# A hybrid decoder layer: recurrence rows moved by DMA, token sums asked for earlier, gate sigmoids kept apart from the decays' exponentials

## The chip, the cores and the metric

The kernel runs on one core of a Trainium2 chip. The core has five engines that run side by side, each with its own queue in a fixed order: TensorE (PE in the profile; it multiplies matrices into banks of PSUM), VectorE (DVE), ScalarE (ACT; it applies functions from tables that it loads), GpSimd (POOL) and SyncE (SP, which here only issues DMAs). They meet at semaphores. The metric is the device time of one execution in microseconds (us); the numbers given are the median of several runs.

## The reference, cut to what matters

One decoder layer on 512 tokens of width 1024, all in float32. A normalised input is projected once into everything that three token mixers and their gates need; the mixers are a gated recurrence with a short convolution (branch 0), chunked gated linear attention (branch 1) and cross-attention to a memory (branch 2). Each mixer's output is projected to the model width, multiplied by a sigmoid gate of its own, and the three are added.

```python
z = rms_norm(x, norm_mix) @ w_in
z_rnn, z_q, z_k, z_v, z_g, z_dec, z_mq, z_gate = split(z)
out_a = rg_lru(causal_dwconv(z_rnn), ...)            # a, u per channel; h_t = a_t h_(t-1) + u_t
log_alpha = log_sigmoid(z_dec @ w_decay + b_decay) / 16
o_gla = chunked_gla(z_q, z_k, z_v, log_alpha)        # cumulated decays, exponentials of them
out_b = rms_norm(o_gla) * silu(z_g)
out_c = softmax(q_mem k_mem / sqrt(d)) v_mem
merged = sum_n sigmoid(z_gate[n]) * (out_n @ w_branch[n])
x = x + merged @ w_out                               # then a gated MLP, and a final norm
```

## The kernel before, in words

**Three matmuls for one.** Every large product is made in a short float format: an operand is split into a high part (a ScalarE copy, L96) and a low part (a VectorE subtraction, L97), and `mm3` (L99) adds hi x hi, hi x lo and lo x hi into one PSUM bank. So each weight block costs a DMA, a ScalarE and a VectorE operation before TensorE can use it. Its high and low parts live in three buffers each (`whi`, `wlo`, NWB = 3), the raw block in four.

**Units and steps.** The program is written down as a list (`prog`) of *units*, weight blocks with their matmuls, and *steps*, other work. `emit` (L182) goes through the list. A unit can ask for functions to be called some units earlier: its load and split two units before (AHEAD = 2), others by the numbers in `pre`. `weave` (L150) spreads steps evenly over units, `blend` (L343) lays the units of a fast product between others. A planner then orders each engine's queue: by the order of the program, but an operation that is ready by the planner's own costs may go ahead of one that isn't. Activations live in 53 slots of 2 KB per partition (`fslot`, `rslot`), and a bank of five in PSUM (`bank`) holds a product until it is read.

**The stage of the change.** Branch 2's units come first, with the recurrence in the steps between: `lru_decay`, `lru_root` and, per block of 96 channels, `lru_scan` (L700), a scan along the tokens on VectorE. Blocks 4 to 7 do not fit the 128-row layout of the projection, so each is cut into three pieces of 32 rows, which ScalarE copies to other partitions (L716, twelve in all). When one of the six tiles is full it is split for TensorE (`oa`).

Then `v_fast` and `g_fast` make the values and the gate of branch 1 by a scheme with seven half-size products in place of eight (`seven`, L284; a1, a2, c1, c2, b1, b2, b3, each of two units). Weights are summed by accumulating DMAs on GpSimd's queue (L298). Sums of token halves are made on VectorE from the normalised input: `h_quarter` (L757) puts a quarter together, `h_sum1` and `h_sum4` (L767, L772) subtract and add them, and `h_ready` splits the result in the same call. `h_sum1` is asked for four units before c1, `h_sum4` five before c2, `h_sum23` four before b1. `v_read` (L794) and `g_read` (L825) empty the banks after each product: L801 and L804 on ScalarE, L805, L809 and the rest on VectorE. `g_read` also calls `silu` (L819), a sigmoid and a product. Seven units of branch 0, gate units (24 matmuls and a sigmoid, L619) and product units (18 matmuls and two VectorE operations, L627 and L628), lie among them: gate 0, gate 1, product 0, product 1, gate 2, product 2, gate 3.

The rest of branch 0 and two held gates of branch 1 (`hold`, L997; sigmoid at L1000) are woven with the decays: `decay_in`, `qk_back` (eight loads of queries and keys by GpSimd), `decay_logit`, `decay_log` (exponentials L883, logarithms L886) and `decay_apply` (L890), which sums the decays along the tokens (L897 to L900) and takes four exponentials per head (L904 to L907) to scale queries and keys (L908 to L913). Six more held gates carry the chunked attention: `k_end` (transposes, L920), `intra`, `state`, `gla_out`, `gla_norm`, `gla_flip`. At the end come the eight products of branch 1.

Of the kernel before, what the change touches and what calls it, by code (L numbers as in the profile page):

```python
# [13 lines left out]
AF = mybir.ActivationFunctionType  # L14
# [4 lines left out]
P = 128  # L19
D = 1024  # L20
KD = D // P
S = 512
NT = S // P
MEM = 256
NMT = MEM // P
MIX = 768
NM = MIX // P
H = 4
DK = 96
# [27 lines left out]
def trunk(ctx: ExitStack, tc: tile.TileContext, x, xT, mem, memT, par, wdecay, wch, wv, wg, wmk,  # L57
# [17 lines left out]
    def fslot(shape=(P, S)):  # L75
        return apool.tile(list(shape), F32, tag="s", name=nm("f"))

    def rslot(shape=(P, S)):
        return apool.tile(list(shape), F32R, tag="s", name=nm("r"))
# [14 lines left out]
    def split(hi, lo, src, eng=None):  # L94

        nc.scalar.activation(hi, src, AF.Copy)  # L96
        (eng or nc.vector).tensor_tensor(out=lo, in0=src, in1=hi.bitcast(F32), op=ALU.subtract)  # L97
# [423 lines left out]
    def proj_in(i, evac):  # L521
        return wch[i], D, lambda w: evac(channel_major(w, KD, lambda k: (hh[:, k, :], hl[:, k, :])))
# [90 lines left out]
    def branch(n, acts, d, gt=None):  # L613

        g = [gt]

        def gate(ps):
            g[0] = fslot()
            nc.scalar.activation(g[0], ps, AF.Sigmoid)  # L619

        def proj(w):
            pp = channel_major(w, NM, lambda k: acts[k])
            if n == BRANCHES[0]:
                merged.append(mslot())
                nc.vector.tensor_tensor(out=merged[d], in0=pp, in1=g[0], op=ALU.mult)
                return
            nc.vector.tensor_tensor(out=g[0], in0=pp, in1=g[0], op=ALU.mult)  # L627
            nc.vector.tensor_tensor(out=merged[d], in0=merged[d], in1=g[0], op=ALU.add)  # L628
            if n == BRANCHES[2]:
                r = (rslot(), rslot())  # L630
                split(*r, merged[d])
                mr.append(r)
        return [proj_in(18 + 8 * n + d, gate), (wbr[n, d], MIX, proj)]
# [66 lines left out]
    def lru_scan(b):  # L700
        a, w = lru.pop(("aw", b))
        gi = lru.pop((1, b))
        nc.vector.tensor_tensor(out=gi, in0=gi, in1=xr[b], op=ALU.mult)
        nc.vector.tensor_tensor(out=w, in0=w, in1=gi, op=ALU.mult)
        if b < 4:
            of.append(fslot())
            gi = of[b][:DK]
        nc.vector.tensor_tensor_scan(out=gi, data0=a, data1=w, initial=0.0, op0=ALU.mult, op1=ALU.add)
        if b < 4:
            return  # L710
        for r in range(3):
            i = 3 * (b - 4) + r
            t, o = (i, DK) if i < 4 else (i // 4 + 3, 32 * (i % 4))
            if t >= 4 and o == 0:
                of.append(fslot())
            nc.scalar.activation(of[t][o:o + 32, :], gi[32 * r:32 * r + 32, :], AF.Copy)  # L716
            if o == DK:
                rr = (rslot(), rslot())
                split(*rr, of[t])
                oa.append(rr)  # L720

    each = lambda fn, bs: [lambda b=b: fn(b) for b in bs]
    lo, hi = range(4), range(4, 8)
# [33 lines left out]
    def h_quarter(r, c, p):  # L757
        f = hsum["f", r, c, p] = fslot((P, 2, HT))
        a, b = (v[:, 4 * c - 4 + 2 * p:4 * c - 2 + 2 * p, (r - 1) * HT:r * HT].bitcast(F32) for v in (hh, hl))
        nc.vector.tensor_tensor(out=f, in0=a, in1=b, op=ALU.add)  # L760
        return f

    def h_ready(key, p, a):
        hsum[key, p] = rslot((P, 2, HT)), rslot((P, 2, HT))
        split(*hsum[key, p], a)

    def h_sum1(p):  # L767
        a, b = h_quarter(2, 1, p), h_quarter(2, 2, p)
        nc.vector.tensor_tensor(out=b, in0=a, in1=b, op=ALU.subtract)
        h_ready("c1", p, b)  # L770

    def h_sum4(p):  # L772
        tt = nc.vector.tensor_tensor
        a, b, s3, s1 = h_quarter(1, 1, p), h_quarter(1, 2, p), hsum["f", 2, 1, p], hsum["f", 2, 2, p]
        tt(out=s3, in0=a, in1=s3, op=ALU.subtract)
        tt(out=a, in0=s1, in1=a, op=ALU.subtract)
        tt(out=b, in0=b, in1=a, op=ALU.add)
        h_ready("c2", p, b)

    def h_sum23(p):  # L780
        h_ready("b1", p, hsum["f", 1, 1, p])
        h_ready("b2", p, hsum["f", 2, 1, p])

    def h_lhs(key, p, j, i):
        tk = slice(i * P, (i + 1) * P)
# [30 lines left out]
            tt(out=flat2(vt[2 + i][0]), in0=k[:, :HP], in1=z, op=ALU.add)  # L816
            tt(out=gla["zd"][:, 2 + i, :], in0=k[:, HP:], in1=ps[:, HP:], op=ALU.add)

    def silu(t, hp, z):  # L819
        s = fslot((P, 2, DV))  # L820
        nc.scalar.activation(flat2(s), z, AF.Sigmoid)
        nc.vector.tensor_tensor(out=flat2(s), in0=flat2(s), in1=z, op=ALU.mult)
        sg[t][hp] = s

    def g_read(key, i, z):  # L825
        tt = nc.vector.tensor_tensor
        if key == "a1":
            gla["g", i] = fslot((P, HP))
            nc.scalar.activation(gla["g", i], z, AF.Copy)
        elif key == "a2":  # L830
            silu(i, 0, z)
        elif key in ("c1", "c2"):
            d = gla["g", key, i] = fslot((P, HP))
            tt(out=d, in0=z, in1=gla["g", i], op=ALU.subtract)
        elif key in ("b1", "b2"):
            d = gla.pop(("g", "c2" if key == "b1" else "c1", i))
            tt(out=d, in0=d, in1=z, op=ALU.subtract)
            silu(i if key == "b1" else i + 2, 1, d)
        else:
            d = gla.pop(("g", i))  # L840
            tt(out=d, in0=d, in1=z, op=ALU.add)
            silu(i + 2, 0, d)

    def v_fast():
        return seven(lambda q, p: wv[p, int(q[1]) - 1, int(q[2]) - 1], HP + LOW, 2, h_lhs,
                     {"c1": [(4, h_sum1)], "c2": [(5, h_sum4)], "b1": [(4, h_sum23)]}, v_read, 4)

    def g_fast():
        return seven(lambda q, p: wg[p, int(q[1]) - 1, int(q[2]) - 1], HP, 2, h_lhs, {}, g_read, 4)
# [39 lines left out]
    dec = const.tile([DK, H, NT], F32, name="dec")  # L889
    qi = []  # L890

    def decay_apply(h):


        by_chunk = lambda a: a.rearrange("p (n c) -> p n c", c=P)
        at = lambda a, i: by_chunk(a)[:, :, i:i + 1].broadcast_to([DK, NT, P])
        nc.vector.tensor_tensor(out=gc[h], in0=gc[h], in1=ea[h], op=ALU.subtract)  # L897
        g = ea[h]
        nc.vector.tensor_tensor_scan(out=g, data0=chm, data1=gc[h], initial=0.0, op0=ALU.mult, op1=ALU.add)
        nc.vector.tensor_tensor(out=by_chunk(gc[h]), in0=at(g, P - 1), in1=by_chunk(g), op=ALU.subtract)  # L900
        m, e, q2 = fslot((DK, S)), fslot((DK, S)), fslot((DK, S))
        nc.vector.tensor_tensor(out=by_chunk(m), in0=by_chunk(g), in1=at(g, CH - 1), op=ALU.subtract)
        with tc.issue_after(gla["last"].ins):
            nc.scalar.activation(gc[h], gc[h], AF.Exp, scale=IG)  # L904
            nc.scalar.activation(q2, g, AF.Exp, scale=IG)
            nc.scalar.activation(e, m, AF.Exp, scale=IG)
            nc.scalar.activation(m, m, AF.Exp, scale=-IG)  # L907
        nc.vector.tensor_tensor(out=gc[h], in0=gc[h], in1=ks[h][:DK], op=ALU.mult)  # L908
        nc.vector.tensor_copy(dec[:, h, :], by_chunk(q2)[:, :, P - 1])
        nc.vector.tensor_tensor(out=q2, in0=q2, in1=qs[h][:DK], op=ALU.mult)  # L910
        qi.append(q2)
        nc.vector.tensor_tensor(out=qs[h][:DK], in0=qs[h][:DK], in1=e, op=ALU.mult)
        nc.vector.tensor_tensor(out=ks[h][:DK], in0=ks[h][:DK], in1=m, op=ALU.mult)  # L913
# [77 lines left out]
        ob.append((hi, lo))  # L991

    step(causal)
    b0 = [u for d in range(KD) for u in branch(0, oa, d)]
    gates = {}

    def hold(d):  # L997
        def evac(ps):
            gates[d] = fslot()
            nc.scalar.activation(gates[d], ps, AF.Sigmoid)  # L1000
        return proj_in(18 + 8 + d, evac)

    held = [hold(d) for d in range(KD)]

    b0 = b0[0:3:2] + [b0[i] for i in range(16) if i not in (0, 2)]
    blend(b0[:7], v_fast() + g_fast())
    weave(b0[7:] + held[:2], [decay_in, qk_back] + [lambda h=h: decay_logit(h) for h in range(H)] + [decay_log] +
          [lambda h=h: decay_apply(h) for h in range(H)])
    tiles = range(NT)
    for u, steps in zip(held[2:], (  # L1010
            each(k_end, tiles) + each(intra, range(H)),
            [lambda n=n, hp=hp: state(n, hp) for n in range(2) for hp in range(2)],
            [lambda hp=hp: state(2, hp) for hp in range(2)] + [lambda t=t: gla_out(t, 0) for t in tiles],
            [lambda: gla_norm(0)] + [lambda t=t: gla_out(t, 1) for t in tiles],
            each(gla_flip, range(3)) + [lambda: gla_norm(1)],
            each(gla_flip, range(3, 6)))):
        weave([u], steps)
    for d in range(KD):
        def late(w, d=d):
            branch(1, ob, d, gates.pop(d))[1][2](w)  # L1020
        weave([(wbr[1, d], MIX, late)], [])


    x2 = [[None, None] for _ in range(NT)]
# [309 lines left out]
```

## Time and profile before

| | us |
|---|---|
| median of 3 runs | 949.54 (948.67 to 950.61) |
| the profiled execution | 949.42 |
| its span, first to last instruction | 947.7 |
| mean granted TensorE clock | 0.993 |
| TensorE busy | 925.9 (98%) |
| VectorE busy | 636.8 (67%) |
| ScalarE busy | 500.4 (53%) |
| GpSimd busy | 83.0 (9%) |

Shares are means over stages with different limits. The rows shown in the prediction have these forms. A *wait* names who waited for whom, then the total, the number of times and the longest. A *group* names line, engine, operation, output<-input, shapes and count, then busy us and mean ns of one, then the engine's idle time before them and what ended it. A *timeline* row gives start, duration and the operation, and in brackets the idle time before it. A row of the *table of stretches* gives the stretch, its length, and busy us (count) of PE, PEld, DVE, ACT and POOL, then granted clock, DMA share and GB/s.

### The profile page before, as it was taken

What the parts mean: (1) busy time and instruction counts of PE and PEld (TensorE: products, weight loads), DVE (VectorE), ACT (ScalarE), POOL (GpSimd) and SP (SyncE); (2) the same over time, 40 slices, a digit from 0 to 9 for tenths busy, and PEclk for the clock granted to TensorE, in tenths of its full rate; (3) what the DMA queues carried; (4) which work ended last, traced back from release to release, by engine and by line L of the source; (5) the groups of instructions that cost most, each with busy time, mean ns of one, the idle gap of its engine ahead of it and who ended that gap; (6) DMA issues with size and microseconds to landing.
All of it is one profiled execution on the core that took longest, in us unless ns stands there. A gap on an engine that the chain in (4) does not pass through costs nothing.

```text
span 947.7 us, 12014 instructions
## 1 busy us (share of the span) xinstructions
PE 925.9 (98%) x4414; PEld 782.4 (83%) x4414; DVE 636.8 (67%) x1111; ACT 500.4 (53%) x806; POOL 83.0 (9%) x115
## 2 busy tenths in 40 slices
PE   8999999999987999999999999999999999999996
PEld 6899888888876998788988898888888888888885
DVE  7897745565777565496767675555585766689765
ACT  7665555584964344696434424433445445445544
POOL 0000000000013151000000000000020221012102
PEclk9999999999998999999999999999999999999999
DMA  7445223223349594322136601323454685357712
GB/s 253 154 124 195 91 77 99 86 72 118 89 99 194 114 217 140 103 71 71 35 117 218 204 17 39 102 90 107 159 104 142 135 222 132 112 114 188 165 45 89
DMA packets 45115, 116.09 MB, mean 122 GB/s; under 512 B 5297, under 2 KB 12609, under 8 KB 45057
## 3 DMA queue, kind: packets, MB, share of 16 engines
q1 hardware_dynamic: 33088, 94.23, 30.5%
q0 software_dynamic: 11392, 20.06, 12.7%
q10 hardware_dynamic: 576, 1.05, 0.3%
q8 instruction: 34, 0.56, 0.2%
q14 instruction: 25, 0.20, 0.1%
HBM read 111.65 MB, written 3.67 MB: 122 GB/s over the span
## 4 chain that ended last, share of the span: by engine, by line
PE 88%; ACT 5%; DVE 5%; issue 1%; DMA 0%; SPq 0%; DVEq 0%; ACTq 0%
PE mm L103 81%; PE sm L103 3%; DVE wlo L97 1%; ACT f L716 1%; PE mm L413 1%; ACT whi L96 1%; DVE r L97 1%; PE sm L957 1%; ACT r L96 0%; DMA m<-in_xT 0%; PE sm L943 0%; PE sm L959 0%; ACT L619 0%; DVE m L381 0%; PE sm L930 0%
## 5 line engine op out<-in xcount | busy, mean ns | idle before, releaser
L97 DVE TENSOR_TENSOR wlo<-raw,whi 128x1024 fp32r<-128x1024 f32 (+2 forms) x155 | 172.0, 1113 | 157.8 <-ACT whi L96 70.1
L96 ACT ACTIVATE whi<-raw 128x1024 fp32r<-128x1024 f32 (+2 forms) x155 | 150.0, 970 | 162.0 <-PE mm L103 148.9
L103 PE MATMUL mm<-whi,r 128*128 128x512 f32 (+2 forms) x568 | 171.9, 373 | 0.0
L103 PE MATMUL mm<-h2l,whi 128*128 128x512 f32 x360 | 140.1, 389 | 0.0
L103 PE MATMUL mm<-h2h,whi 128*128 128x512 f32 x360 | 139.9, 389 | 0.0
L103 PEld LDWEIGHTS mm<-whi,r 128*128 128x128 f32 x568 | 106.4, 189 | 15.4 <-issue 0.3
L103 PE MATMUL mm<-hh,whi 128*128 128x512 f32 x288 | 114.7, 398 | 3.0 <-ACT whi L96 3.0
L103 PE MATMUL mm<-hl,whi 128*128 128x512 f32 x288 | 113.7, 395 | 0.0
L103 PE MATMUL mm<-wlo,r 128*128 128x512 f32 (+2 forms) x284 | 106.3, 374 | 0.2 <-DVE wlo L97 0.2
L103 PE MATMUL mm<-r,whi 128*128 128x512 f32 (+1 forms) x448 | 100.3, 373 | 6.3 <-DVE f L805 6.3
L103 PEld LDWEIGHTS mm<-r,whi 128*128 128x128 f32 x448 | 78.6, 191 | 21.4 <-issue 7.4
L103 PE MATMUL mm<-h2h,wlo 128*128 128x512 f32 x360 | 88.9, 389 | 0.0
L96 ACT ACTIVATE whi<-f 128x512 fp32r<-128x512 f32 (+2 forms) x90 | 48.2, 580 | 74.9 <-PE mm L103 62.9
L97 DVE TENSOR_TENSOR wlo<-f,whi 128x512 fp32r<-128x512 f32 (+2 forms) x90 | 53.9, 632 | 38.4 <-PE mm L103 21.1
L103 PEld LDWEIGHTS mm<-h2h,wlo 128*128 128x128 f32 x360 | 67.6, 188 | 14.0
L103 PEld LDWEIGHTS mm<-h2l,whi 128*128 128x128 f32 x360 | 67.6, 188 | 14.0
L103 PEld LDWEIGHTS mm<-h2h,whi 128*128 128x128 f32 x360 | 67.5, 188 | 13.9
L1098 DVE SCALAR_TENSOR_TENSOR f<-mm,prm,f 128x511 f32<-128x511 f32 x96 | 71.4, 745 | 6.9 <-ACT f L1096 6.1
L298 POOL DMA_DIRECT2D f<-in_wdown x40 | 35.2, 981 | 435.9 <-DMA f<-in_wdown 290.9
L103 PE MATMUL mm<-hh,wlo 128*128 128x512 f32 x288 | 71.9, 390 | 0.0
L103 PEld LDWEIGHTS mm<-hh,whi 128*128 128x128 f32 x288 | 54.7, 190 | 15.2 <-ACT whi L96 3.3
L103 PEld LDWEIGHTS mm<-hl,whi 128*128 128x128 f32 x288 | 54.7, 190 | 11.1
(233 smaller groups left out, 1317.4 us busy)
## 6 DMA issues: line engine op xcount, KB each, us to landing
raw<-in_wup SPq DMA_DIRECT2D x48, 512.0 KB, 3.6
raw<-in_wch SPq DMA_DIRECT2D x40, 512.0 KB, 3.5
f<-in_wdown POOLq DMA_DIRECT2D x40, 256.0 KB, 5.5
raw<-in_wbr SPq DMA_DIRECT2D x24, 384.0 KB, 3.2
raw<-in_wdown SPq DMA_DIRECT2D x14, 512.0 KB, 3.6
f<-in_wdown SPq DMA_DIRECT2D x20, 256.0 KB, 5.0
raw<-in_wout SPq DMA_DIRECT2D x8, 512.0 KB, 3.5
f<-in_wv POOLq DMA_DIRECT2D x16, 200.0 KB, 5.0
```

What stands on the lines that cost most here:

```text
L96: nc.scalar.activation(hi, src, AF.Copy)
L97: (eng or nc.vector).tensor_tensor(out=lo, in0=src, in1=hi.bitcast(F32), op=ALU.subtract)
L103: nc.tensor.matmul(ps, lhsT=l, rhs=r, start=first and i == 0, stop=last and i == len(seq) - 1, skip_group_check=more)
L298: nc.gpsimd.dma_start(raw[to, p][j], src(q, p)[:, j, :], accum_op=ALU.add)
L413: nc.tensor.matmul(ps[u], lhsT=a, rhs=b, start=q == 0 and i in (0, 2), stop=q == KD - 2 and i >= len(seq) - 2)
L716: nc.scalar.activation(of[t][o:o + 32, :], gi[32 * r:32 * r + 32, :], AF.Copy)
L957: nc.tensor.matmul(ps[:, j, :], lhsT=sT[h][:, t, :], rhs=vt[t][hp][:, j, :], start=True, stop=t == 0)
L1098: nc.vector.scalar_tensor_tensor(out=a[:, j:], in0=ps[:, :S - j], scalar=col(C_FCW + 48 * (2 - j) + f), in1=a[:, j:], op0=ALU.mult, op1=AL ...
```

## The change

- `lru_scan` moves its pieces with twelve DMAs on GpSimd's queue in place of ScalarE copies. The splits become steps of their own (`lru_out`), three behind product a2 and three behind product c2 of `v_fast`.
- `h_sum1` and `h_sum4` only make the sums, and are asked for seven units before c1 and c2. `h_ready` is asked for two units before c1, c2, b1 and b2; `h_sum23` is gone.
- `g_read` leaves the gate's input in slots; `silu` is called in the state stage, four times behind `intra` and four times ahead of the last `state`.
- Gate 2 and product 1 change places. Gates 4 to 7 of branch 0 come together, woven with `decay_in`, logits, logarithms and the decays' sums (`decay_sum`, taken out of `decay_apply`); products 3 to 7 follow, woven with `qk_back` and `decay_apply`. All eight held gates of branch 1 carry the chunked attention, whose steps are spread over eight units in place of six.

```diff
-            nc.scalar.activation(of[t][o:o + 32, :], gi[32 * r:32 * r + 32, :], AF.Copy)
-            if o == DK:
-                rr = (rslot(), rslot())
-                split(*rr, of[t])
-                oa.append(rr)
+            nc.gpsimd.dma_start(of[t][o:o + 32, :], gi[32 * r:32 * r + 32, :])
+
+    def lru_out(t):
+        oa.append((rslot(), rslot()))
+        split(*oa[t], of[t])
...
-    def h_ready(key, p, a):
-        hsum[key, p] = rslot((P, 2, HT)), rslot((P, 2, HT))
+    def h_ready(key, p):
+        a, hsum[key, p] = hsum[key, p], (rslot((P, 2, HT)), rslot((P, 2, HT)))
         split(*hsum[key, p], a)
...
         a, b = h_quarter(2, 1, p), h_quarter(2, 2, p)
+        hsum["c1", p] = b
         nc.vector.tensor_tensor(out=b, in0=a, in1=b, op=ALU.subtract)
-        h_ready("c1", p, b)
...
-        h_ready("c2", p, b)
-
-    def h_sum23(p):
-        h_ready("b1", p, hsum["f", 1, 1, p])
-        h_ready("b2", p, hsum["f", 2, 1, p])
+        hsum["c2", p], hsum["b1", p], hsum["b2", p] = b, a, s3
...
-    def silu(t, hp, z):
+    def silu(t, hp):
+        z = gla.pop(("z", t, hp))
...
     def v_fast():
+        pre = {k: [(2, lambda p, k=k: h_ready(k, p))] for k in ("c1", "c2", "b1", "b2")}
+        pre["c1"].append((7, h_sum1))
+        pre["c2"].append((7, h_sum4))
         return seven(lambda q, p: wv[p, int(q[1]) - 1, int(q[2]) - 1], HP + LOW, 2, h_lhs,
-                     {"c1": [(4, h_sum1)], "c2": [(5, h_sum4)], "b1": [(4, h_sum23)]}, v_read, 4)
+                     pre, v_read, 4)
...
-    def decay_apply(h):
+    def decay_sum(h):
         nc.vector.tensor_tensor(out=gc[h], in0=gc[h], in1=ea[h], op=ALU.subtract)
         g = ea[h]
         nc.vector.tensor_tensor_scan(out=g, data0=chm, data1=gc[h], initial=0.0, op0=ALU.mult, op1=ALU.add)
         nc.vector.tensor_tensor(out=by_chunk(gc[h]), in0=at(g, P - 1), in1=by_chunk(g), op=ALU.subtract)
+
+    def decay_apply(h):
+        g = ea[h]
         m, e, q2 = fslot((DK, S)), fslot((DK, S)), fslot((DK, S))
...
-    blend(b0[:7], v_fast() + g_fast())
-    weave(b0[7:] + held[:2], [decay_in, qk_back] + [lambda h=h: decay_logit(h) for h in range(H)] + [decay_log] +
-          [lambda h=h: decay_apply(h) for h in range(H)])
+    g0, p0 = [hold(0, d) for d in range(KD)], [held(0, oa, d) for d in range(KD)]
+    g1 = [hold(1, d) for d in range(KD)]
+    blend(g0[:2] + p0[:1] + g0[2:3] + p0[1:3] + g0[3:4], v_fast() + g_fast(), each(lru_out, range(NM)) + [lambda: None] * 15)
+    weave(g0[4:], [decay_in] + each(decay_logit, heads) + [decay_log] + each(decay_sum, heads))
+    weave(p0[3:], [qk_back] + each(decay_apply, heads))
+    for u, steps in zip(g1, (
+            each(k_end, tiles),
+            each(intra, heads) + [lambda t=t: silu(t, 0) for t in tiles],
...
+    weave([held(1, ob, d) for d in range(KD)], [])
```

More of the change, by code (lines that the diff above doesn't have):

```diff
@@ L826, in g_read @@
         tt = nc.vector.tensor_tensor
[L827 to L831, printed above, removed]
+        if key in ("a1", "a2"):
+            d = gla[("g", i) if key == "a1" else ("z", i, 0)] = fslot((P, HP))
+            nc.scalar.activation(d, z, AF.Copy)
         elif key in ("c1", "c2"):
-            d = gla["g", key, i] = fslot((P, HP))
+            d = gla["z", i + 2 if key == "c1" else i, 1] = fslot((P, HP))
             tt(out=d, in0=z, in1=gla["g", i], op=ALU.subtract)
         elif key in ("b1", "b2"):
-            d = gla.pop(("g", "c2" if key == "b1" else "c1", i))
+            d = gla["z", i if key == "b1" else i + 2, 1]
             tt(out=d, in0=d, in1=z, op=ALU.subtract)
-            silu(i if key == "b1" else i + 2, 1, d)
         else:
-            d = gla.pop(("g", i))
+            d = gla["z", i + 2, 0] = gla.pop(("g", i))
             tt(out=d, in0=d, in1=z, op=ALU.add)
-            silu(i + 2, 0, d)
     def v_fast():
+        pre = {k: [(2, lambda p, k=k: h_ready(k, p))] for k in ("c1", "c2", "b1", "b2")}
+        pre["c1"].append((7, h_sum1))
+        pre["c2"].append((7, h_sum4))
         return seven(lambda q, p: wv[p, int(q[1]) - 1, int(q[2]) - 1], HP + LOW, 2, h_lhs,
-                     {"c1": [(4, h_sum1)], "c2": [(5, h_sum4)], "b1": [(4, h_sum23)]}, v_read, 4)
+                     pre, v_read, 4)
     def g_fast():
@@ L890, in trunk @@
     qi = []
-    def decay_apply(h):
-        by_chunk = lambda a: a.rearrange("p (n c) -> p n c", c=P)
-        at = lambda a, i: by_chunk(a)[:, :, i:i + 1].broadcast_to([DK, NT, P])
+    by_chunk = lambda a: a.rearrange("p (n c) -> p n c", c=P)
+    at = lambda a, i: by_chunk(a)[:, :, i:i + 1].broadcast_to([DK, NT, P])
+    def decay_sum(h):
         nc.vector.tensor_tensor(out=gc[h], in0=gc[h], in1=ea[h], op=ALU.subtract)
@@ L993, in trunk, with hold, held @@
     step(causal)
-    b0 = [u for d in range(KD) for u in branch(0, oa, d)]
     gates = {}
-    def hold(d):
+    def hold(n, d):
         def evac(ps):
[L999 to L1005, printed above, removed]
-    blend(b0[:7], v_fast() + g_fast())
-    weave(b0[7:] + held[:2], [decay_in, qk_back] + [lambda h=h: decay_logit(h) for h in range(H)] + [decay_log] +
-          [lambda h=h: decay_apply(h) for h in range(H)])
-    tiles = range(NT)
-    for u, steps in zip(held[2:], (
-            each(k_end, tiles) + each(intra, range(H)),
+            gates[n, d] = fslot()
+            nc.scalar.activation(gates[n, d], ps, AF.Sigmoid)
+        return proj_in(18 + 8 * n + d, evac)
+    def held(n, acts, d):
+        return wbr[n, d], MIX, lambda w: branch(n, acts, d, gates.pop((n, d)))[1][2](w)
+    g0, p0 = [hold(0, d) for d in range(KD)], [held(0, oa, d) for d in range(KD)]
+    g1 = [hold(1, d) for d in range(KD)]
+    tiles, heads = range(NT), range(H)
+    blend(g0[:2] + p0[:1] + g0[2:3] + p0[1:3] + g0[3:4], v_fast() + g_fast(), each(lru_out, range(NM)) + [lambda: None] * 15)
[4 more added lines that the diff above has]
+            each(intra, heads) + [lambda t=t: silu(t, 0) for t in tiles],
             [lambda n=n, hp=hp: state(n, hp) for n in range(2) for hp in range(2)],
-            [lambda hp=hp: state(2, hp) for hp in range(2)] + [lambda t=t: gla_out(t, 0) for t in tiles],
-            [lambda: gla_norm(0)] + [lambda t=t: gla_out(t, 1) for t in tiles],
+            [lambda t=t: silu(t, 1) for t in tiles] + [lambda hp=hp: state(2, hp) for hp in range(2)] +
+            [lambda t=t: gla_out(t, 0) for t in range(2)],
+            [lambda t=t: gla_out(t, 0) for t in range(2, 4)] + [lambda t=t: gla_out(t, 1) for t in range(2)],
+            [lambda: gla_norm(0)] + [lambda t=t: gla_out(t, 1) for t in range(2, 4)],
             each(gla_flip, range(3)) + [lambda: gla_norm(1)],
@@ L1017, in trunk @@
         weave([u], steps)
[L1018 to L1021, printed above, removed]
+    weave([held(1, ob, d) for d in range(KD)], [])
     x2 = [[None, None] for _ in range(NT)]
```

## The prediction

> **What bounds the kernel now.** I read the page's totals first, then what TensorE waited for, then a table of stretches, then the order of the work inside the three stretches where TensorE stood.
>
> ```profile
> PE 925.9 (98%) x4414; PEld 782.4 (83%) x4414; DVE 636.8 (67%) x1111; ACT 500.4 (53%) x806; POOL 83.0 (9%) x115
> ...
> PE mm L103 <- DVE f L805: 6.3, 1, 6.3
> PE mm L103 <- ACT whi L96: 3.0, 1, 3.0
> PE sm L920 <- DVE f L908: 1.5, 1, 1.5
> ...
> 240.00:250.00 10.00, 10.00 (x45) 8.26 (x45) 4.89 (x8) 9.93 (x15) 0.00 (x0) 1.00 0.28 84
> 250.00:300.00 50.00, 40.76 (x176) 35.27 (x176) 40.76 (x63) 32.13 (x53) 11.78 (x14) 0.90 0.61 144
> 300.00:360.00 60.00, 60.00 (x312) 55.76 (x311) 36.66 (x64) 25.25 (x46) 20.88 (x27) 1.00 0.74 161
> ```
>
> The columns of the last three rows are the stretch, its length, busy time (and count) of PE, PEld, DVE, ACT, POOL, the granted clock, the DMA share and GB/s. TensorE is busy 925.9 of 947.7 us, so the change can only win where it stands. Between 250 and 300 us it stands 50 - 40.76 = 9.2 us, and its clock of 0.90 stretches the 40.76 us that it works by about 40.76 x 0.10 = 4.1 us. That is 13.3 us in one stage, and the stage after it has no idle at all. The 1.5 us at L920 are the third place. So at most **13.3 + 1.5 = 14.8 us** are to be had in the part of the program that the change touches.
>
> ```profile
> 271.15 0.50 PE L103 MATMUL mm<-hh,whi 128*128 128x512 f32 x1 [2.98 <-ACT whi L96]
> ...
> 272.38 0.63 PE L103 MATMUL mm<-hh,whi 128*128 128x512 f32 x1
> 272.81 0.63 PE L103 MATMUL mm<-hl,whi 128*128 128x512 f32 x1
> ...
> 293.65 3.33 PE L103 MATMUL mm<-r,whi 128*128 128x512 f32 x7 [6.26 <-DVE f L805]
> ...
> 293.60:299.10 5.50, 5.45 (x14) 4.79 (x15) 3.48 (x7) 2.42 (x5) 1.67 (x2) 0.50 0.98 332
> ```
>
> The 4.1 us belong to the stops: after each, matmuls start 0.43 us apart (272.38 to 272.81) instead of half that; behind the second, the clock is 0.50 for 5.45 us of work, so 2.7 of the 4.1 us are there. The Trainium skill, page "TensorE: Matmul & The Clock Gate", section "What's actually happening", halves the clock only after an idle window of about 3.4 us; by that rule the stop of 2.98 us would have cost no clock, and here it did, so the trace disagrees. By the rule a leftover stop under 3.4 us would add nothing to my sum; by the row it could add 1 to 2 us, a share like that of the first stop.
>
> **First stop.** ScalarE's queue, then VectorE's part of the same stage:
>
> ```profile
> L96 ACT ACTIVATE r<-f 128x512 fp32r<-128x512 f32 x14 | 8.4, 629 | 8.7 <-DVE f L777 5.6 <-DVE f L769 3.0
> L716 ACT ACTIVATE f<-f 32x512 f32<-32x512 f32 x12 | 7.5, 629 | 0.2
> ...
> 266.19 2.55 ACT L716 ACTIVATE f<-f 32x512 f32<-32x512 f32 x4
> 270.06 1.04 ACT L96 ACTIVATE whi<-raw 128x1024 fp32r<-128x1024 f32 x1
> ...
> L760 DVE TENSOR_TENSOR f<-hh,hl 128x512 f32<-128x512 f32 x8 | 5.2, 687 | 0.0
> L809 DVE TENSOR_TENSOR f<-mm,f 128x384 f32<-128x384 f32 x4 | 2.1, 553 | 0.0
> ...
> 262.55 1.22 DVE L708 TENSOR_TENSOR_SCAN f<-f,f 96x512 f32<-96x512 f32 x1
> ```
>
> The twelve copies that shift rows between partitions (L716) hold ScalarE for 7.5 us just ahead of the weight split that TensorE waits for (270.06). **Second stop**, the same queue 22 us later:
>
> ```profile
> 292.06 0.63 ACT L96 ACTIVATE r<-f 128x512 fp32r<-128x512 f32 x1 [3.79 <-DVE f L777]
> 292.60 0.85 ACT L804 ACTIVATE f<-mm 128x384 f32<-128x384 f32 x2
> ```
>
> ScalarE reached the split of a token sum and stood 3.79 us until VectorE had made the sum (L777). Behind it in the queue is L804, which empties the accumulators of product a2; TensorE wants one of those banks for the next unit. L805 is VectorE's part of that read, itself behind the sums.
>
> **The change, part by part.** My sum is made against the profiled execution, 949.42 us (span 947.7 and 1.72 around it); the median of the runs is 949.54, so I add 0.1 at the end.
>
> *Copies to DMAs.* ScalarE loses twelve of 0.629 us, 7.5 us, against a stop of 2.98. The twelve DMAs join GpSimd's queue, where the weight sums (L298) are also issued. No row shows a 32-row DMA between two places on chip; the nearest are these:
>
> ```profile
> L557 POOL DMA_DIRECT2D qk<-f x8: 514/514/716, 115.6 to 167.6; - x8
> ...
> qk<-f POOLq DMA_DIRECT2D x8, 192.0 KB, 2.7
> f<-qk POOLq DMA_DIRECT2D x8, 192.0 KB, 3.2
> f<-in_wv POOLq DMA_DIRECT2D x16, 200.0 KB, 5.0
> ```
>
> Issue lies between nothing and 0.72 us; I take 0.51, 6.2 us for twelve on an engine that is busy 11.78 of 50. Landing lies between nothing and 5.0 us; I take 3.2, the plain copy being nearer than the accumulating one. The last scan ends at 263.8, its three pieces are issued by 265.3 and land by 268.5. The splits of the six tiles (a ScalarE and a VectorE operation each, as before) now come behind product a2, so they should not wait. A weight sum queued behind three pieces is 1.5 us later; c1's are asked for six units early (units of 2.2 us, a row under the rivals; about 13 us), which hides that, and would cost the 1.5 us without it. So the first stop goes, and its slow clock.
>
> *Token sums.* No operation is added: eight L760 and eight sums of the same size (L769, L775 to L777; 0.69 us each) are asked for two or three units sooner, and their splits later. The 8.7 us that ScalarE stood for them (row of r<-f, 5.6 and 3.0) vanish, and with them the second stop. What is late next is VectorE. It works 40.76 us in a stage that would shrink to 50 - 13.3 = 36.7, so **4.1 us** too many, and the two reads of c1's banks (L809, 0.55 each, 1.1 together), which c2 needs empty, stand in the same queue. I take a leftover of 4.1 + 1.1 = **5.2 us**. The bounds: zero, if the sums slip into VectorE's 5.1 free us between 240 and 250, or splits into the 23 free us after 300; all 13.3, if the queue keeps its order. I stay near the low end because the surplus in busy time is a row and the rest is order.
>
> *Silu and unit order.* Eight sigmoids (L821) and their products (L822) move to the state stage:
>
> ```profile
> 437.00:560.00 123.00, 123.00 (x611) 104.97 (x610) 83.56 (x182) 50.45 (x103) 0.00 (x0) 1.00 0.37 117
> ...
> L821 ACT ACTIVATE f<-f 128x384 f32<-128x384 f32 x6 | 3.1, 521 | 3.5 <-DVE f L837 2.3 <-DVE f L841 1.2
> L822 DVE TENSOR_TENSOR f<-f,f 128x384 f32<-128x384 f32 x6 | 3.3, 554 | 0.1
> ```
>
> There TensorE never stands, VectorE has 39 us free and ScalarE 73. The two reads of a2 become copies of the same size, so ScalarE gains two operations, about 1 us. Cost nothing; uncovered, 8 x (0.52 + 0.55) = 9 us. Gate 2 ahead of product 1 swaps two units with the same matmuls: nothing.
>
> *Decays.* In 380 to 440 us, ScalarE:
>
> ```profile
> L1000 ACT ACT_TABLE_LOAD x4 | 5.1, 1283 | 0.1
> L883 ACT ACT_TABLE_LOAD x3 | 3.8, 1283 | 0.1
> L619 ACT ACT_TABLE_LOAD x3 | 3.8, 1283 | 0.1
> ...
> 388.51 4.31 PE mm L103 x18
> ...
> 445.32 5.47 PE mm L103 x24
> ...
> 404.00:433.00 29.00, 27.48 (x130) 22.73 (x129) 28.38 (x43) 27.54 (x36) 2.04 (x4) 1.00 0.22 73
> ...
> L97 DVE TENSOR_TENSOR wlo<-raw,whi 128x1024 fp32r<-128x1024 f32 x5 | 6.1, 1216 | 0.0
> ```
>
> Every gate sigmoid (L619, L1000) among exponentials brings a table load of 1.28 us and another back. With all branch-0 gates ahead and branch-1 gates behind, the sixteen exponentials of L904 to L907 run in one piece: at least the four loads of L1000 and their four returns go, 10 us. But 28.38 of 29 us on VectorE say that it is just as full here, and its work stays. What helps it is that the sums (L897 to L900) now start under the four gate units. What hurts is cover: k_end's transposes came behind three gate units (16.4 us), now behind one (5.47). From the start of gate 4 to k_end TensorE has 4 x 5.47 + 5 x 4.31 + 5.47 = 49 us and four logits. VectorE's 28.38, three more products with two operations of about 0.69, like the sums (4.1) and the four gate units' splits at 1.2 make 37. It fits, so the 1.5 us go; bounds are a gain of 1.5 and the loss in the third rival.
>
> **Sum.** 949.42 - 13.3 - 1.5 + 5.2 = 939.8, with 0.1: **939.9 us**.
>
> **Rivals.**
>
> *Everything goes* (VectorE's surplus finds its free time): 949.5 - 14.8 = **934.7**. For it, the 28 free us on both sides; against, splits have only three buffers, so they cannot be made much ahead.
>
> *A transfer takes the second stop's place.* Product b2's second weights are loaded and summed late:
>
> ```profile
> 277.89 0.35 PE L103 MATMUL mm<-whi,hh 128*128 128x400 f32 x1
> ...
> 282.27 0.62 PE L103 MATMUL mm<-hh,wlo 128*128 128x512 f32 x2
> ...
> 291.11 0.91 SPq L293 DMA_DIRECT2D f<-in_wv  x2
> ...
> 297.43 1.76 POOL L298 DMA_DIRECT2D f<-in_wv  x2 [8.86 <-DMA f<-in_wv]
> ...
> 309.42 0.42 PE L103 MATMUL mm<-whi,r 128*128 128x400 f32 x1
> ```
>
> Issue at 297.4, landing 5.0 and a split put them at about 304 (ScalarE and VectorE, 2 x 2 x 0.5, like L809: 2). Product a2, two units, runs from 277.89 to 282.27, so a unit takes 2.2. TensorE begins b2 at 309.4 and its second unit 2.2 later; 13.3 sooner that is 298.3. Were the load not to move, a stop of 6 with 2.7 of slow clock comes in place of the leftover: 949.5 - 14.8 + 8.7 = **943.4**. Against it: the load waits for slots and buffers that faster work frees sooner.
>
> *The decays become the stop.* If the sums start only once gate 7 is done, VectorE has 28.38 + 4.1 = 32.5 us of work over 5 x 4.31 + 5.47 = 27.0: a stop of 5.5 and 2.7 of slow clock in place of 1.5, so 939.9 + 1.5 + 6.7 = **948.1**, no change that can be told. Against it: the logarithms need only the logits, which come behind gates 4 and 5.
>
> *Slower: ScalarE waits for the pieces.* If the planner puts the splits of the recurrence tiles right behind their DMAs, ScalarE stands at each of the four groups for three issues and a landing, with the weight splits behind. At 3.2 us of landing that is 4 x 4.7 = 19 us, at 4.1 (midway between the plain and the accumulating rows) 4 x 5.6 = 22.4, in place of 7.5 of copies: TensorE loses 14.9 more in the first stop and 6.3 + 2.7 + 1.5 = 10.5 less behind it, 949.5 + 14.9 - 10.5 = **953.9**. It decides from waits of 7.5 + 10.5 = 18 us in all. For it: a planner that takes landing as shorter than it is. The Trainium skill, page "SBUF — State Buffer", section "SBUF: two separate sides", in its note on the "DVE blocks DMA" trap, says that a GpSimd DMA cannot write its descriptors while VectorE runs a two-port copy, which would stretch these waits; the stage's VectorE rows above are two-input sums and scans, so no row here shows it. Against it: the splits stand behind product a2, about 9 us later.
>
> **Chances and range.** Forecast 0.44, everything goes 0.13, the transfer 0.15, the decays 0.13, ScalarE waits 0.15. About 0.2% (1.9 us) is what can be told from no change. The first three are faster, 0.72; the decays are the same, 0.13; the last is slower, 0.15. The forecast's own range is 936 to 943. The range goes from 934 (nothing left of the stops) to 951.5, which leaves out the slower case alone.
>
> **What would show it.** Right: no L716 on ScalarE, no stop over 2 us at 268 and 287, the r splits with no idle behind L769 and L777, VectorE near 10 in 10 between 255 and 295, ScalarE's L904 to L907 with one table load, no wait at L920. Wrong: a wait of TensorE for a recurrence tile's split or for b2's weights, k_end waiting for L908, or clock rows under 1.00 behind a new stop. The prediction falls if VectorE's surplus shows as many stops with slow clock, or as none.

## The result, and the profile after

The changed kernel takes **940.61 us** (median of 4 runs, 939.67 to 941.68) against 949.61 (948.67 to 950.61) for the kernel before, run beside it: a ratio of 0.9905, 95% interval 0.9888 to 0.9923. The forecast was 939.9. The profiled execution took 939.67 us with a span of 938.0, so 9.75 us less than the one the forecast started from.

First the totals of the changed kernel's page, then its waits of TensorE (who waited for whom, total us, times, longest), then its table of stretches (stretch, length, busy us and count of PE, PEld, DVE, ACT, POOL, granted clock, DMA share, GB/s).

```profile
PE 921.4 (98%) x4414; PEld 779.6 (83%) x4414; DVE 635.1 (68%) x1111; ACT 485.9 (52%) x791; POOL 88.8 (9%) x127
```

```profile
PE mm L103 <- ACT whi L96: 3.3, 3, 1.1
PE sm L921 <- DVE f L909: 2.2, 1, 2.2
...
PE mm L103 <- DVE r L97: 0.4, 1, 0.4
```

```profile
250.00:260.00 10.00, 10.00 (x46) 8.28 (x45) 10.00 (x16) 6.55 (x11) 3.60 (x7) 1.00 0.47 121
260.00:270.00 10.00, 8.85 (x44) 7.76 (x43) 9.38 (x15) 4.60 (x7) 7.26 (x12) 1.00 0.79 159
270.00:280.00 10.00, 10.00 (x52) 9.23 (x51) 9.76 (x18) 5.13 (x11) 4.40 (x7) 1.00 0.77 205
280.00:290.00 10.00, 8.65 (x46) 7.74 (x45) 7.94 (x14) 5.13 (x9) 2.88 (x4) 1.00 1.12 248
290.00:300.00 10.00, 8.85 (x44) 7.46 (x43) 9.86 (x19) 7.08 (x13) 3.23 (x4) 1.00 0.83 182
```

In the stage from 250 to 300 us TensorE now stands 1.15 + 1.35 + 1.15 = 3.65 us in place of 9.2, and no row is below a clock of 1.00, where the whole stage had 0.90. The two long stops (2.98 and 6.26) are gone; what is left is four short ones. This stage alone gives 13.3 - 3.65 = 9.65 us, nearly all of the 9.75. The third stop, at the transposes of `k_end`, did not go: it grew from 1.5 to 2.2 us (its line is L921 now). These two make 9.65 - 0.7 = 9.0; the other 0.8 us I did not trace to a place.

In the changed kernel's timeline of TensorE, the stops with their releasers:

```profile
268.74 0.50 PE L103 MATMUL mm<-hh,whi 128*128 128x512 f32 x1 [1.15 <-ACT whi L96]
...
285.06 0.96 PE L103 MATMUL mm<-r,whi 128*128 128x512 f32 x3 [0.98 <-ACT whi L96]
...
299.59 0.50 PE L103 MATMUL mm<-hh,whi 128*128 128x512 f32 x1 [1.15 <-ACT whi L96]
...
412.15 0.47 PE L921 MATMUL sm<-ident,f 96*128 96x96 f32 x3 [2.18 <-DVE f L909]
```

Three of the four leftovers in the stage wait for the high part of a weight block, not for a token sum. The twelve transfers and the splits, in the view of the one line L716, the list of DMA issues, and the groups of ScalarE between 250 and 300 us:

```profile
L716 POOL DMA_DIRECT2D f<-f x12: 496/518/536, 255.8 to 264.8; - x12
...
DMA to landing us min/median/max: 1.8/2.1/2.9
```

```profile
L96 ACT ACTIVATE r<-f 128x512 fp32r<-128x512 f32 x14 | 8.0, 620 | 0.0
```

One issue takes 0.518 us (the first triple is minimum, median and maximum in ns), landing 2.1. ScalarE no longer stands ahead of the splits of the sums: 0.0 us of idle where there were 8.7.

### The profile page after: what moved, and what is told of

It reads as the page before. It is cut to its first block, busy times and chain, and to the rows that moved or that the text cites. A ratio compares the mean times of both kernels' runs of the same rounds, so it can differ in the third digit from the quotient of the medians.

```text
span 938.0 us, 12024 instructions
## 1 busy us (share of the span) xinstructions
PE 921.4 (98%) x4414; PEld 779.6 (83%) x4414; DVE 635.1 (68%) x1111; ACT 485.9 (52%) x791; POOL 88.8 (9%) x127
## 4 chain that ended last, share of the span: by engine, by line
PE 85%; DVE 7%; ACT 3%; issue 2%; DMA 1%; POOL 0%; SPq 0%; ACTq 0%; DVEq 0%; POOLq 0%
PE mm L103 79%; PE sm L103 2%; DVE wlo L97 1%; DMA f<-in_wv 1%; PE mm L413 1%; DVE r L97 1%; PE sm L958 1%; DMA m<-in_xT 0%; PE sm L944 0%; PE sm L960 0%; DVE m L381 0%; PE sm L931 0%; DVE f L895 0%; ACT whi L96 0%; PE sm L1084 0%
## 5 line engine op out<-in xcount | busy, mean ns | idle before, releaser
L298 POOL DMA_DIRECT2D f<-in_wdown x40 | 35.1, 987 | 440.9 <-DMA f<-in_wdown 292.8
```

Of the source, the lines that this page charges most:

```text
L298: nc.gpsimd.dma_start(raw[to, p][j], src(q, p)[:, j, :], accum_op=ALU.add)
```

## The experiments

My theory was that the two stops of the stage have two causes (copies ahead of a weight split; a sum not yet made) and that the sums' order on VectorE decides what is left. The rivals were that ScalarE's queue is one cause behind both, that the leftover has another cause, and that the third part does not pay. Each run is compared with runs of the kernel before on the same chip (medians 949.0 to 949.2).

### The layout by DMA alone

On the kernel before:

```diff
-            nc.scalar.activation(of[t][o:o + 32, :], gi[32 * r:32 * r + 32, :], AF.Copy)
-            if o == DK: ... split(*rr, of[t])
+            nc.gpsimd.dma_start(of[t][o:o + 32, :], gi[32 * r:32 * r + 32, :])
+    def lru_out(t): ...                    # a step of its own, as in the change
```

> The kernel before with the first part alone: recurrence pieces moved by DMA, their splits as steps behind a2 and c2; sums, silu and decays as before. Theory of separate stops: the first stop (2.98 us and 1.7 of slow clock) goes, the second (6.3 and 2.7) and the third (1.5) stay: 945. Rival of one queue: ScalarE only reaches the wait for the token sums sooner and stands there longer, so the second stop grows by about what the first gives back: 948.5 to 949.5, with a second stop of 9 us or more.

Measured: 945.22 us, ratio 0.9959 (0.9944 to 0.9974), a gain of 3.8. Its timeline of TensorE:

```profile
269.37 0.50 PE L103 MATMUL mm<-hh,whi 128*128 128x512 f32 x1 [1.21 <-ACT whi L96]
286.47 0.60 PE L856 MATMUL sm<-ident,f 128*16 128x128 f32 x2 [2.61 <-DVE f L805]
```

The first stop fell from 2.98 to 1.21 us, and the time is the 945 that the theory of separate stops expected, but not by its mechanism: the second also fell, from 6.26 to 2.61, though no sum was asked for earlier. The last of the sums in the timelines of VectorE, of the kernel before and of this one:

```profile
291.34 0.69 DVE L777 TENSOR_TENSOR f<-f,f 128x512 f32<-128x512 f32 x1
```

```profile
284.14 0.69 DVE L777 TENSOR_TENSOR f<-f,f 128x512 f32<-128x512 f32 x1
```

In the kernel before, VectorE made the low parts of six recurrence tiles ahead of the sums, and stood 2.40 us, until 269.66, for a weight piece that ScalarE had made behind its copies; here these splits come later, and the first sum (L769) starts at 267.02 in place of 273.85. So the two stops are not independent: what stands ahead of the first in the queues of ScalarE and VectorE also delays the sums.

### The earlier sums alone

On the kernel before, `h_sum1`, `h_sum4`, `h_ready` and the `pre` numbers of `v_fast` as in the change; the twelve copies stay on ScalarE.

> The kernel before with the second part alone: token sums asked for seven units ahead, their splits two; copies and decays as before. Theory of separate stops: the second stop (6.3 and 2.7) goes, the first stays at about 3 us with slow clock: 940.7 to 941.5. Rival of one queue: the sums crowd VectorE where the copies crowd ScalarE, the first stop grows to 6 us or more: 944 to 947.

Measured: 940.71 us, ratio 0.9917 (0.9897 to 0.9938). This part alone brings 8.3 us, nearly as much as the whole change. In its timeline of ScalarE four copies still stand ahead of the same weight split; the second view has what followed the same four copies in the kernel before:

```profile
265.73 0.85 ACT L96 ACTIVATE whi<-raw 128x800 fp32r<-128x800 f32 x1
266.61 2.55 ACT L716 ACTIVATE f<-f 32x512 f32<-32x512 f32 x4
269.18 1.06 ACT L96 ACTIVATE whi<-raw 128x1024 fp32r<-128x1024 f32 x1
```

```profile
268.76 0.87 ACT L96 ACTIVATE whi<-raw 128x800 fp32r<-128x800 f32 x1
269.54 0.61 ACT L96 ACTIVATE r<-f 128x512 fp32r<-128x512 f32 x1
```

TensorE's stop there was 1.57 us, in place of 2.98, and the idle time in 250 to 300 us is 50 - 46.24 = 3.76, where the whole change has 3.65. Taking 7.5 us of copies off ScalarE was therefore not needed for most of this. Nor did ScalarE wait for sums ahead of the first stop: in the kernel before it had no idle time from 250 to 271 us. What changed is its order. Another weight split (265.73) now goes ahead of the four copies, and the split of a recurrence tile goes behind, so the split that TensorE wants starts 0.88 us sooner (269.18 against 270.06). TensorE also arrives 0.55 us later, having stood 0.53 us for a low part at 266.34.

### The third part alone

On the kernel before, the order of the units, `decay_sum`, and the late `silu`, without the other two parts.

> The kernel before with the third part alone: gates ahead of the decays' exponentials, silu late, one held gate before k_end in place of three; copies and sums as before. Theory that VectorE's order sets k_end: the third stop stays between 1.5 and 3 us, time 949 to 951. Rival that table loads set it: ScalarE's 10 us fewer of loads end the third stop, 947.5 to 948.2.

Measured: 950.19 us, ratio 1.0012 (1.0000 to 1.0025). Its waits of TensorE:

```profile
PE mm L103 <- DVE f L805: 6.2, 1, 6.2
PE mm L103 <- ACT whi L96: 3.0, 1, 3.0
PE sm L922 <- DVE f L910: 2.2, 1, 2.2
```

The two large stops are untouched and the third grew to 2.2 us. The part brings nothing here, and the growth from 1.5 to 2.2 us that the changed kernel shows comes from it, not from faster work ahead.

### The first two parts without the third

> The kernel before with the layout by DMA and the earlier sums, and without the third part. If the third part costs what it cost alone (0.7 us, a longer stop at k_end), this is faster than the whole change: 939.9 and a stop there of about 1.5 us. If the third part is needed once the sums come earlier (the gates' sigmoids between the decays then hold ScalarE up), it is slower than the whole change: 941.5 or more. If the parts bring nothing beyond the sums, 940.7 as the sums alone.

The kernel before with the two edits above. Measured: 939.63 us (939.38 to 939.73), ratio 0.9897 (0.9880 to 0.9914), with the stop at `k_end` back at 1.53 us. From its waits of TensorE:

```profile
PE sm L919 <- DVE f L907: 1.5, 1, 1.5
```

The median is 1.0 us below that of the whole change, but the intervals overlap; that the third part costs something is likely (it came out so both alone and here), its size is not settled. Together with the runs above, by the medians: copies 3.8, sums 8.3, both 9.6 us. So about 2.5 us of what each brings alone is the same lost time. That the copies add something to the sums is likely but not settled, as the intervals of the sums alone and of both overlap.

### The splits right behind their transfers

On the changed kernel, to put the slower rival in force:

```diff
             nc.gpsimd.dma_start(of[t][o:o + 32, :], gi[32 * r:32 * r + 32, :])
+            if o == DK:
+                rr = (rslot(), rslot())
+                split(*rr, of[t])
+                oa.append(rr)
-    blend(..., v_fast() + g_fast(), each(lru_out, range(NM)) + [lambda: None] * 15)
+    blend(..., v_fast() + g_fast())
```

> The changed kernel, with the splits of the recurrence tiles written right behind their DMAs, where the copies had theirs. Rival of the prediction that ScalarE then waits for the pieces: idle of 10 us or more before r splits of recurrence tiles, 946 or more. Theory that landing is short (2.1 us in the changed kernel) and ScalarE has 20 idle us in this stage: under 3 us of such idle, 940 to 943.

Measured: 946.04 us, ratio 0.9977 (0.9966 to 0.9987), by the medians 5.4 us slower than the changed kernel, with intervals clear of each other. In the view of line L716, then in the timelines of GpSimd, ScalarE and TensorE of this kernel:

```profile
L716 POOL DMA_DIRECT2D f<-f x12: 496/804/847, 256.0 to 270.1; - x12
...
  ACT r L96: 7.5, 3
...
DMA to landing us min/median/max: 1.8/5.1/7.5
```

```profile
263.77 0.86 POOL L298 DMA_DIRECT2D f<-in_wv  x1 [3.50 <-ACT r L96]
...
266.60 4.28 POOL L716 DMA_DIRECT2D f<-f  x8
```

```profile
274.46 0.63 ACT L96 ACTIVATE r<-f 128x512 fp32r<-128x512 f32 x1 [5.54 <-DMA f<-f]
...
278.74 0.89 ACT L797 ACTIVATE f<-mm 128x400 f32<-128x400 f32 x2
```

```profile
279.29 0.70 PE L103 MATMUL mm<-whi,hh 128*128 128x400 f32 x1 [4.59 <-ACT f L797]
```

The rival's mechanism is real. A weight sum (L298) that waits 3.50 us for ScalarE stands in GpSimd's queue ahead of eight pieces; these are issued late and land late (median 5.1 us, not 2.1); ScalarE stands 5.54 us at a split of theirs; and L797, which empties a bank, is queued behind, so TensorE stands 4.59. Its size was overrated: ScalarE waited 7.5 us in all, where the rival had 19 or more. What keeps the change clear of it is the place of the splits behind the products.

### The eight sums left out

On the changed kernel, `h_sum1` and `h_sum4` without their additions and subtractions (the quarters themselves are used).

> The changed kernel with the eight subtractions and additions of token sums left out (the quarters are still put together and split, but c1, c2, b1 and b2 multiply plain quarters, so branch 1's values and gates are others): VectorE has 8 x 0.6 = 4.8 us less in the stage from 250 to 300. Theory of the prediction, a surplus of VectorE: the leftover of 3.65 us in that stage falls to under 1, time 937 to 938. Rival, the three weight buffers and the order of units: the stops on weight splits at about 268, 285 and 299 stay near 1 us each, leftover 3 to 4, time 940 to 941.

Measured: 939.10 us, ratio 0.9892 (0.9870 to 0.9913). Its stretches:

```profile
250.00:300.00 50.00, 46.64 (x226) 40.85 (x225) 43.05 (x69) 28.75 (x50) 21.20 (x30) 1.00 0.78 183
...
372.00:376.00 4.00, 4.00 (x12) 3.13 (x12) 2.52 (x4) 3.97 (x6) 0.00 (x0) 0.60 0.32 89
```

VectorE has about 4 us less to do, and TensorE still stands 50 - 46.64 = 3.36 us, 0.3 less than with the sums. Two of the three waits for a weight block's high part stay (1.15 and 0.93 us); in place of the third come two short ones for splits of the quarters (0.57 and 0.71). So the leftover in this stage is not VectorE's surplus, as my forecast had it. The stop at `k_end` fell to 0.60 us in this run, but VectorE is hardly earlier there (0.28 us); in the timelines of this kernel and of the changed one, the product that the transposes wait for:

```profile
411.14 0.68 DVE L905 TENSOR_TENSOR f<-f,f 96x512 f32<-96x512 f32 x1
```

```profile
411.42 0.67 DVE L909 TENSOR_TENSOR f<-f,f 96x512 f32<-96x512 f32 x1
```

It is TensorE that arrived 1.3 us later, having run 4 us at a clock of 0.60 (4 x 0.40 = 1.6 us, as much as the stop is shorter). What it loses ahead of a point that VectorE sets, it does not lose again at the stop.

### Four weight buffers, with a control

Three of the leftovers wait for a high part, and ScalarE makes that high part only when TensorE has let go of a buffer. In the changed kernel's timeline of ScalarE, the split ahead of the stop at 268.74:

```profile
267.63 1.06 ACT L96 ACTIVATE whi<-raw 128x1024 fp32r<-128x1024 f32 x1 [0.82 <-PE mm L103]
```

So I gave the blocks a fourth buffer. It needs room, which is taken from the slots; the control has the fewer slots alone.

```diff
-NSLOT = 53
-NWB = 3
+NSLOT = 49
+NWB = 4          # the control keeps 3
```

> The changed kernel with four buffers for the high and low weight parts in place of three, and 49 activation slots in place of 53 to pay for them. Theory of buffers: a split can be made three units ahead, the stops on weight splits between 250 and 300 go, leftover under 1.5 us against its control with three buffers and 49 slots. Theory of a surplus of VectorE: leftover stays at 3 us or more, no difference from the control.

> Control for four buffers: the changed kernel with 49 activation slots and three buffers. If slots matter little here: 940 to 942; if they set the order of the sums and loads: 943 or more.

Measured: 937.57 us, ratio 0.9880 (0.9856 to 0.9903), with four; 940.61, ratio 0.9910 (0.9886 to 0.9934), for the control. The two intervals overlap, but all four times with the fourth buffer (936.53 to 939.31) lie below all four of the control (939.52 to 941.68). The stage in the one and in the other:

```profile
250.00:300.00 50.00, 48.93 (x239) 43.25 (x238) 48.10 (x78) 29.77 (x52) 21.93 (x30) 1.00 0.76 172
```

```profile
250.00:300.00 50.00, 46.45 (x225) 40.51 (x223) 46.98 (x76) 28.99 (x50) 21.35 (x30) 1.00 0.79 182
```

The idle time falls from 3.55 to 1.07 us, and the stops of 1.15 us at 268 and 299 are gone from the timeline. VectorE does more in the same 50 us (48.10), and of the stops left there (0.71 and 0.35 us) only the short one waits for it. The leftover is thus mostly the release of the weight buffers. What is won is not lost again as a longer stop at `k_end`: TensorE gets there 2.6 us sooner than in the changed kernel, the product that it waits for is 2.7 us sooner, and the stop is 2.09 us; behind it, this profile has a clock of 0.57 for 4 us.

### The keys ahead of the other decays

In the changed kernel the exponential and the product that `k_end` needs (L905 and L909) are taken out of `decay_apply` and asked for first, for all heads:

```diff
+    def decay_k(h):
+        with tc.issue_after(gla["last"].ins):
+            nc.scalar.activation(gc[h], gc[h], AF.Exp, scale=IG)
+        nc.vector.tensor_tensor(out=gc[h], in0=gc[h], in1=ks[h][:DK], op=ALU.mult)
...
-    weave(p0[3:], [qk_back] + each(decay_apply, heads))
+    weave(p0[3:], [qk_back] + each(decay_k, heads) + each(decay_apply, heads))
```

> The changed kernel with the decays' step for the keys of k_end (one exponential and one product per head) ahead of the rest of decay_apply, for all four heads. Theory that VectorE's order sets k_end: the wait of 2.2 us at k_end's transposes goes, no wait over 0.5 us comes at intra, time 938 to 939. Rival that VectorE is simply full there: the wait moves to intra's products (which need the scaled queries and keys), 940 to 941.

Measured: 939.42 us, ratio 0.9908 (0.9877 to 0.9939). Its waits of TensorE, and its timeline of ScalarE:

```profile
PE sm L924 <- ACT f L926: 1.6, 1, 1.6
```

```profile
413.60 0.63 ACT L911 ACTIVATE f<-f 96x512 f32<-96x512 f32 x1 [2.40 <-DVE f L908]
414.25 1.28 ACT L1003 ACT_TABLE_LOAD   x1
```

The product L901 of the last head is now made by 398.5, and nothing waits for it. In its place the transposes wait for ScalarE's copy of the first ones (L926), whose queue holds an exponential that stands 2.40 us for VectorE (L908), and two table loads with a sigmoid between them. The stop is 0.6 us shorter, and its cause is the same: VectorE is late with the decays, and whichever engine comes next in order passes that on. By the intervals this time can't be told from that of the change.

### Both mends, and the fourth buffer without the third part

> The changed kernel with a fourth weight buffer (49 slots) and with the exponential and product of the keys ahead of the rest of the decays. If the two leftovers are separate waits, the gains add: 940.6 - 3.0 - 1.2 = 936.4, no wait on a whole weight piece over 1 us left in 250 to 300, and at the transposes of k_end the 1.6 us of the keys run. If VectorE is the one limit behind both, what is saved at 268 to 300 comes back in the decays, where VectorE is full: not below the fourth buffer alone, 937.6, with the stop at k_end longer than 2.1 us.

> The kernel of copies_and_sums with a fourth weight buffer and 49 slots. If the waits on whole weight pieces at 268 to 300 are those of the buffers whatever the decays do, the fourth buffer takes 3.0 us here too: 936.9. If the order of the decays decides what it is worth, the gain comes out under 1 us: 939 or more.

The first is the changed kernel with the last two edits: **936.99 us** (936.54 to 938.59), ratio 0.9868 (0.9847 to 0.9889), the lowest median of all, though its interval overlaps that of the fourth buffer alone. Its row of the stage:

```profile
250.00:300.00 50.00, 48.91 (x240) 43.38 (x239) 48.10 (x78) 28.77 (x52) 22.03 (x30) 1.00 0.76 173
```

The idle time in 250 to 300 us is 1.09, the stop at `k_end` 1.67. So what was won at 250 to 300 did not come back as a longer stop in the decays, though the clock behind that stop was 0.74 from 413 to 418 us. The sum of the single gains (936.4) lies just below, within what can be told. The second is `copies_and_sums` with the fourth buffer: 938.00 us (936.99 to 939.55), ratio 0.9882 (0.9861 to 0.9902). There the buffer took 1.6 us of median where 3.0 were expected; the idle time in the stage fell as before, 3.40 to 1.09, but in the profiled execution the stop at `k_end` went from 1.53 to 2.02 us and a slow clock came behind it (0.83 between 420 and 430). There part of what was won early was given back.

## Why the prediction was right, and where it was not

**Right: the total and its main term.** The 13.3 us of the stage, 9.2 idle and 4.1 of slow clock, were the place, and both long stops and all of their slow clock went. The forecast was 0.7 us off the median. It was partly luck: the leftover was 1.5 us smaller than forecast and the third stop 2.2 us worse, and the 0.8 us that I did not trace lie the other way again.

**The first stop: right that it goes, wrong that only the copies could take it away.** The step said that the stop goes because ScalarE loses 7.5 us of copies "just ahead of the weight split". Only four of the twelve (2.55 us) stood next ahead, with two other splits (0.87 and 0.61 us) between them and it. `sums_only` keeps the copies and has 1.57 us of stop; `copies_only` has 1.21, the whole change 1.15. Either edit mends about half of it or more, the one by the copies' time, the other by another order of ScalarE's queue.

**The twelve transfers.** Issue was taken at 0.51 us and is 0.518. Landing was taken at 3.2 (bounds 0 to 5.0), from transfers of 192 KB, and is 2.1 for these of 64 KB. Neither moved the sum, as the splits stand far behind.

**The second stop: right.** The 8.7 us that ScalarE stood for the sums are 0.0, and VectorE is near 10 in 10 as foreseen, but for the row from 280 to 290 (7.94).

**The leftover: sized at 5.2, measured 3.65, and its cause was wrong.** The step that failed is "It works 40.76 us in a stage that would shrink to 50 - 13.3 = 36.7", which made 4.1 us too many (the other 1.1, for the reads of c1's banks, are no wait of TensorE either). Busy time of VectorE in this stretch was no floor for it: `no_half_sums` takes 4 us of it away and keeps 3.36 us of the leftover; `four_buffers` leaves it in and keeps 1.07. The cause is the three buffers of a weight block, which the forecast named only as an argument against "everything goes".

**The third stop: wrong.** "It fits, so the 1.5 us go" counted VectorE's 37 us of work against the 49 us in which TensorE goes from gate 4 to `k_end`. In the changed kernel's table of stretches and its timelines of VectorE and ScalarE:

```profile
352.00:384.00 32.00, 31.96 (x145) 25.57 (x144) 16.02 (x22) 22.50 (x29) 3.05 (x6) 1.00 0.38 113
384.00:413.00 29.00, 26.82 (x127) 22.09 (x126) 29.00 (x46) 20.09 (x28) 1.93 (x4) 1.00 0.32 109
```

```profile
379.01 0.69 DVE L893 TENSOR_TENSOR f<-f,f 96x512 f32<-96x512 f32 x1 [2.24 <-ACT f L882]
...
382.86 1.29 DVE L893 TENSOR_TENSOR f<-f,f 96x512 f32<-96x512 f32 x2 [1.18 <-ACT f L882]
```

```profile
379.00 1.28 ACT L1000 ACT_TABLE_LOAD   x1
380.29 0.60 ACT L1000 ACTIVATE f<-mm 128x512 f32<-128x512 f32 x1
380.90 1.28 ACT L882 ACT_TABLE_LOAD   x1
...
411.57 1.28 ACT L1000 ACT_TABLE_LOAD   x1
...
413.48 1.28 ACT L908 ACT_TABLE_LOAD   x1
```

The work does fit, but it could not start: the sums (L893) wait for ScalarE's logarithms (L882), which share ScalarE with the gates' sigmoids and pay a table load for each return. So VectorE works 16.02 of 32 us and then 29.00 of 29, and the last head's product is late. The condition of the rival "the decays become the stop" nearly held: the sum of one head began under gate 7, at 379.01, the others as that gate ended, from 382.86 on. Its price was 5.5 us of stop and 2.7 of clock, and the stop is 2.2, without slow clock in this profile. `k_end` waiting for the keys' product was one of the signs of being wrong that the prediction named. The step "the sixteen exponentials run in one piece" failed too: a sigmoid of branch 1 stands between the third and the fourth of the last head (411.57 and 413.48), and between 360 and 425 us ScalarE has eleven table loads, where the kernel before had sixteen between 380 and 440. Five loads of 1.283 us went, 6.4 us in place of 10.

**The rivals.** "Everything goes" (934.7) asked for what only a fourth buffer came near to in that stage. The transfer of b2's weights never held TensorE. The slower rival is real where the splits stand behind their transfers (946.04 against 953.9 forecast), and the change as made avoids it for the reason given.

## What to carry to other kernels

Where an engine with a fixed order stands for something that its own next neighbour makes late, ask for that thing sooner before taking work away from the engine: here the order brought 8.3 us, and the moved copies by the medians 1.3 more. A cause read off a busy share (more work than the stage is long) is to be tested by taking the work away; here that left the stop standing, and another buffer removed it. Whoever gathers work to save table loads should look at what then comes due at once on the engine behind.

## What the runs showed that I had not expected

**The clock does not follow the length of the stop alone.** The control with fewer slots has nearly the same stop at `k_end` as the changed kernel, 2.19 and 2.18 us. In the tables of stretches, the control and then the changed kernel:

```profile
413.00:417.00 4.00, 4.00 (x12) 3.09 (x12) 3.62 (x5) 3.87 (x7) 0.00 (x0) 0.57 0.50 154
```

```profile
412.00:416.00 4.00, 3.85 (x19) 3.13 (x20) 4.00 (x7) 3.96 (x6) 0.00 (x0) 1.00 0.39 126
```

One lost 4 x 0.43 = 1.7 us of clock, the other nothing. In other profiles a stop of 2.09 us was followed by a clock of 0.57 over 4 us (`four_buffers`), one of 1.67 by 0.74 over 5 us (`buffers_and_keys`), and one of 1.61 by none below 1.00 (`keys_first`). The run without the sums fell to 0.60 at 372 us behind no stop that its timeline shows, in a stretch with the small matmuls of the logits. The Trainium skill, page "TensorE: Matmul & The Clock Gate", section "What's actually happening", halves the clock after an idle window of about 3.4 us, and says that the windows run freely, so that their phase differs from run to run. That one stop costs clock in one execution and none in another agrees with the second; that stops of 2.98 and 2.19 us, shorter than a window, and no stop at all were followed by slow clock does not agree with the first. What decides it I can't say.

**The same transfers landed at two speeds.** The same twelve transfers of 64 KB landed in 2.1 us (median; at most 2.9) in the changed kernel, and in 5.1 us (median; up to 7.5) where eight of them were issued in a row behind a weight sum that had been held up; their issue went from 0.518 to 0.804 us. Which part of that is the queue and which the load of the DMA engines was not tried.
